# Prompt keys and values of a hybrid decoder layer: from TensorE transposes to VectorE squares and reordering stores

## The chip, the cores and the metric

The kernel runs on one core of one Trainium2 chip. A core has five engines that each work through their own list of instructions in order: TensorE (PE, with its weight loads as PEld), VectorE (DVE), ScalarE (ACT), GpSimd (POOL) and SyncE (SP). SP computes nothing here; it issues nearly all transfers, which then run on the core's 16 DMA engines. The metric is the device time of one execution in microseconds. Three timed runs of the kernel before took 1741.89 to 1742.96 us, with a median of 1742.4 us.

## The reference, cut to what matters

One decoder layer runs over a prompt of 1024 tokens and a sample of 8 sequences with 4 new tokens each, in one program (1056 tokens). From the normalised input a projection makes, among others, the stick-breaking q, k and v (8 heads of 64), the DeltaNet inputs and two gates. The prompt's keys and values are used by attention and are also outputs.

```python
def decoder_layer(x, ...):                          # once for the prompt, once for the sample
    p = rmsnorm(x, norm_mix_w) @ w_in
    q_a, k_a, v_a, u, z, a, b, g_a, g_b = jnp.split(p, ...)
    o_a = sb_prompt(q_a, k_a, v_a, sb_bias)         # w[q,k] = beta * product of (1-beta) after k; o = w @ v
    o_b, ssm_new = gdn_branch(short_conv(u_ext, conv_w), z, a, b, ...)   # gated delta rule, 4 heads
    m = sigmoid(g_a) * (o_a @ w_pa) + sigmoid(g_b) * (o_b @ w_pb)
    x = x + m @ w_o
    x = x + square(relu(rmsnorm(x, norm_mlp_w) @ w_up)) @ w_down
    return x, k_a, v_a, conv_new, ssm_new
# outputs, among others: k_a and v_a of the prompt as (page of 128 tokens, token, head, 64)
```

## The kernel before

Activations lie transposed in SBUF: features on the 128 partitions, tokens along the free dimension. Float32 products are made from a rounded part and a remainder of each factor, so that `dense` (L134) issues three matmuls (L137, L138, L139) for each 128 rows of the sum. `load_w` (L118) fetches 128 columns of weights through a staging tile that exists once (`wst`), and ACT and DVE split it into two tiles of which two pairs exist.

The front half of the program, up to some 890 us, has these parts in the text: four DeltaNet heads (`gdn_head`, L379), each with its projections, a chain through small transfers to DRAM and back (`ms_d` at L454, L456; 31 steps on DVE at L464; `tv_d` at L467, L471) and eight dependent chunks (L538, matmuls y, s, o); the sample's DeltaNet step; the projections of stick-breaking q, k and v (loop at L783, pair of heads p by pair, evacuated by `ev`, L793); the sample's attention (L854: scores dsc, transposed weights dwt, values dav, and dos, whose result `osT` is stored at L906); and the prompt's attention (`pipeline`, L1028), whose first stage `stage_a` loads a head's q and k (`attn_load`, L914) and, for every second head, v (`load_v`, L964), and makes scores (sc). Gate projections (pd_g, `gate_steps`, L1037; 16 jobs of 4 chunks with 24 matmuls each) and the transposed residual input (xrp, `residual_step`, L1046) are work that depends on none of these. Eleven gate jobs are written ahead of attention, the other five as fill between its blocks. After that come the merge, the output projection and the channel mixer, from some 890 us to the end.

The order on each engine is not the order of the text. A scheduler builds the program with a time model of its own and takes, engine by engine, what is ready first, within the limits of the pools: a tile's next user waits for the last reader of the buffer it takes over. The list of each engine is then fixed. Two such limits matter here. The projections of q, k, v, the gates and xrp share two PSUM tiles (`psf`, through `dtile(..., True)`) that are handed on in the order of the text, so gate chunk 1 of the job g1_5 can't be placed before the residual xrp0, which stands ahead of it. And attention's tiles (pool `ak`, L911) take the place of the sample's (pool `bk`, closed at L907), so they can't be filled before the sample's attention is over. SP's list is in order too: a transfer that waits for something holds up every transfer behind it.

For k and v of each pair p, the projection leaves a tile f of 128 features x 1024 tokens. Eight TensorE transposes (`tr8`, L367) turn it into two PSUM tiles t_nk or t_nv, ACT copies these into `nt` (L809), and SP stores `nt` to the output (L811) and, for v, once more to the scratch tensor `v_d` (L813), from which `load_v` reads later.

Of the kernel before, what the change touches and what calls it, by code (L numbers as in the profile page):

```python
# [8 lines left out]
F32 = mybir.dt.float32  # L9
# [9 lines left out]
P = 128  # L19
D = 1024  # L20
NP = 1024
# [17 lines left out]
def hybrid_step(ctx, tc, x_prompt, x_sample, cache_k, cache_v, page_table, state_conv, state_ssm,  # L39
# [24 lines left out]
    def dtile(name, f=False):  # L64
        if f:
            return psf.tile([P, 512], F32, tag="f", name=name)
        return psd.tile([P, 512], F32, tag="d", name=name)
# [80 lines left out]
    z_d = dr.tile([GH, P, NP], F32, name="z_d")  # L148
    q_d = [dr.tile([4, P, NP], F32, name=f"q{x}_d") for x in "hl"]
    k_d = [dr.tile([4, P, NP], F32, name=f"k{x}_d") for x in "hl"]  # L150
    v_d = dr.tile([4, P, NC, P], F32, name="v_d")
    cg_d = dr.tile([GH, NC, P], F32, name="cg_d")
    ms_d = dr.tile([GH, 4, NC, 32, 32], F32, name="ms_d")
    tv_d = dr.tile([GH, 4, NC, 32, 32], F32, name="tv_d")
# [221 lines left out]
    def c8(ap):  # L376
        return ap.rearrange("p (c f) -> p c f", f=P)
# [405 lines left out]
    for p in range(4):  # L783
        for nm, col, keep_s in (("q", 0, qsT), ("k", 512, ksT), ("v", 1024, vsT)):
            hi = lo = f = None
            if nm != "q":
                f = fk.tile([P, T], F32, tag="ft", name=f"{nm}f{p}", bufs=NFT)
            if nm != "v":
                hi = fk.tile([P, NP], F32R, tag="ft", name=f"{nm}h{p}", bufs=NFT)
            if nm == "q":  # L790
                lo = fk.tile([P, NP], F32, tag="ft", name=f"{nm}l{p}", bufs=NFT)

            def ev(c, o, n, pt, f=f, hi=hi, lo=lo, keep_s=keep_s[:, p, :]):  # L793
                m = min(n, NP - o)
                with tc.high_priority():
                    if hi is not None:
                        S_.activation(hi[:, o:o + m], pt[:, :m], AF.Copy)
                    if lo is not None:
                        V.tensor_tensor(lo[:, o:o + m], pt[:, :m], hi[:, o:o + m].bitcast(F32), op=ALU.subtract)
                    if f is not None:  # L800
                        S_.activation(f[:, o:o + m], pt[:, :m], AF.Copy)
                    if m < n:
                        V.tensor_copy(keep_s, pt[:, m:n])

            proj([(col + p * P, f"a{nm}{p}", ev)], f=True)
            if nm != "q":
                nt = fk.tile([P, NP], F32, tag="ft", name=f"nt{nm}{p}", bufs=NFT)
                for hf, pt in enumerate(tr8(f, f"n{nm}{p}", lambda n_: dtile(n_, True))):
                    S_.activation(nt[:, hf * 512:(hf + 1) * 512], pt, AF.Copy)  # L809
                dst = nk_prompt if nm == "k" else nv_prompt  # L810
                SY.dma_start(dst[0, 0, :, :, 2 * p:2 * p + 2, :].rearrange("c t h d -> t c (h d)"), c8(nt))  # L811
                if nm == "v":
                    SY.dma_start(v_d[p], c8(nt))  # L813
            if nm == "k":
                lo = f[:, 0:NP]
                V.tensor_tensor(lo, lo, hi.bitcast(F32), op=ALU.subtract)
            if nm != "v":
                for dst, src in zip(q_d if nm == "q" else k_d, (hi.bitcast(F32), lo)):
                    SY.dma_start(dst[p], src)
# [143 lines left out]

    def load_v(p):  # L964
        vn = ak.tile([P, NC, P], F32, tag="vn", name=f"vn{p}", bufs=2)
        SY.dma_start(vn, v_d[p])
        return vn

    def values_of(blk):
# [39 lines left out]
    def stage_a(x):  # L1009
        if x >= NB:  # L1010
            return
        hh, _ = blks[x]
        if hh not in heads:
            if hh // 2 not in vns:
                vns[hh // 2] = load_v(hh // 2)
            heads[hh] = attn_load(hh)
        state[x] = scores(blks[x])

    def stage_b(x, fill):
# [648 lines left out]
```

## Time and profile before

| | us |
|---|---|
| timed runs, median of three (lowest to highest) | 1742.4 (1741.89 to 1742.96) |
| the profiled execution | 1736.88 |
| its span, from the first to the last instruction | 1735.2 |
| mean granted TensorE clock | 0.993 of full speed |
| PE busy | 1689.5 (97% of the span) |
| DVE busy | 1143.6 (66%) |
| ACT busy | 781.7 (45%) |
| POOL busy | 198.2 (11%) |

Rows of the profile name an instruction by its line, its engine, its operation and `out<-in` with the program's tile names. "Idle before, releaser" is the time in which an engine stood still ahead of an instruction and what ended it. A matmul's own duration (some 280 ns) is longer than the distance to the next one, since they overlap; the distance is what the work costs.

### The profile page before, as it was taken

To read this page: it belongs to the slowest core of one execution; us is meant where nothing else is said; L and a number is where in the kernel's file an instruction comes from. 1 tells how busy PE (TensorE), PEld (TensorE's weight loads), DVE (VectorE), ACT (ScalarE), POOL (GpSimd) and SP (SyncE) were. 2 spreads that over 40 slices of the span, in tenths; PEclk is the share of its full clock that TensorE was granted. 3 is DMA by queue.
4 is the path that set the end of the run, shared out by engine and by line. 5 is a ranking of instruction groups with operands and counts; after the bars stand their busy time and mean duration, and the time that the engine had idled before them with its cause. 6 is when DMAs were issued, how large, how long until landed. Compare 5 with 4: busy or idle time off the path is not lost.

```text
span 1735.2 us, 34777 instructions
## 1 busy us (share of the span) xinstructions
PE 1689.5 (97%) x14030; PEld 1631.0 (94%) x14030; DVE 1143.6 (66%) x2300; ACT 781.7 (45%) x1560; POOL 198.2 (11%) x243
## 2 busy tenths in 40 slices
PE   7999999999999989999999999999999999999998
PEld 6999999999998778887989999999999999999998
DVE  6665677867243317558757487887776778788843
ACT  5453434343324225545433356554445564344353
POOL 2110111110005214335200000000000000000000
PEclk9999999999999999999999999999999999999999
DMA  5132233234446576748134644545443666442321
GB/s 179 37 120 76 68 106 92 85 119 135 123 132 216 149 194 172 194 124 241 57 113 126 184 139 144 158 133 160 151 155 113 235 220 214 155 132 94 122 81 66
DMA packets 234220, 239.24 MB, mean 138 GB/s; under 512 B 22882, under 2 KB 192195, under 8 KB 234060
## 3 DMA queue, kind: packets, MB, share of 16 engines
q1 hardware_dynamic: 229110, 226.27, 43.0%
q0 software_dynamic: 3200, 10.52, 1.9%
q8 instruction: 110, 1.80, 0.4%
q10 hardware_dynamic: 1750, 0.23, 0.1%
q14 instruction: 50, 0.41, 0.1%
HBM read 163.21 MB, written 73.77 MB: 137 GB/s over the span
## 4 chain that ended last, share of the span: by engine, by line
PE 77%; DVE 6%; issue 6%; DMA 6%; POOL 3%; ACT 2%; SPq 0%; POOLq 0%; DVEq 0%; ACTq 0%
PE pu L139 6%; PE pu L137 6%; PE pu L138 6%; PE pw L139 4%; PE pw L138 4%; PE pw L137 4%; PE pd_g L137 2%; PE pd_g L139 2%; PE pd_g L138 2%; POOL am L943 2%; PE px L138 1%; PE px L137 1%; PE px L139 1%; PE pv L139 1%; PE pv L137 1%
## 5 line engine op out<-in xcount | busy, mean ns | idle before, releaser
L139 PE MATMUL pu<-Xh,ul 128*128 128x264 f32 x812 | 230.1, 284 | 0.0
L137 PE MATMUL pu<-Xh,uh 128*128 128x264 f32 x812 | 229.8, 283 | 0.3 <-ACT uh L1231 0.3
L138 PE MATMUL pu<-Xl,uh 128*128 128x264 f32 x812 | 229.7, 283 | 0.0
L137 PE MATMUL pw<-hc,w 128*128 128x264 f32 x728 | 205.9, 285 | 2.4 <-ACT w L1480 2.4
L138 PE MATMUL pw<-hc,w 128*128 128x264 f32 x728 | 206.1, 286 | 0.0
L139 PE MATMUL pw<-hc,w 128*128 128x264 f32 x728 | 201.3, 285 | 0.2 <-DVE w L1481 0.2
L137 PEld LDWEIGHTS pu<-Xh,uh 128*128 128x128 f32 x812 | 153.1, 189 | 0.5 <-ACT uh L1231 0.5
L138 PEld LDWEIGHTS pu<-Xl,uh 128*128 128x128 f32 x812 | 152.7, 188 | 0.0
L139 PEld LDWEIGHTS pu<-Xh,ul 128*128 128x128 f32 x812 | 152.0, 188 | 0.0
L137 PE MATMUL pd_g<-xh,wh_g 128*128 128x256 f32 (+1 forms) x512 | 150.4, 294 | 0.0
L139 PE MATMUL pd_g<-xh,wl_g 128*128 128x256 f32 (+1 forms) x512 | 149.1, 291 | 0.0
L138 PE MATMUL pd_g<-xl,wh_g 128*128 128x256 f32 (+1 forms) x512 | 148.7, 290 | 0.0
L137 PEld LDWEIGHTS pw<-hc,w 128*128 128x128 f32 x728 | 138.0, 190 | 2.7 <-ACT w L1480 2.6
L138 PEld LDWEIGHTS pw<-hc,w 128*128 128x128 f32 x728 | 137.3, 189 | 0.0
L139 PEld LDWEIGHTS pw<-hc,w 128*128 128x128 f32 x728 | 134.6, 188 | 0.4 <-DVE w L1481 0.4
L947 DVE TENSOR_TENSOR_SCAN pr<-am 128x127 f32<-128x127 f32 (+7 forms) x64 | 88.0, 1376 | 62.5 <-POOL am L943 62.4
L139 PEld LDWEIGHTS pd_g<-xh,wl_g 128*128 128x128 f32 x512 | 97.5, 190 | 3.1 <-issue 2.9
L137 PEld LDWEIGHTS pd_g<-xh,wh_g 128*128 128x128 f32 x512 | 97.6, 191 | 2.9 <-issue 2.1
L138 PEld LDWEIGHTS pd_g<-xl,wh_g 128*128 128x128 f32 x512 | 97.4, 190 | 1.0 <-issue 0.8
L1480 ACT ACTIVATE w<-a 128x512 fp32r<-128x512 f32 x78 | 43.4, 620 | 85.9 <-PE pw L139 77.6
L139 PE MATMUL px<-mh,wl_wo 128*128 128x264 f32 x256 | 72.3, 285 | 1.2 <-DVE wl_wo L1232 1.1
L138 PE MATMUL px<-ml,wh_wo 128*128 128x264 f32 x256 | 72.6, 285 | 0.0
(579 smaller groups left out, 5083.4 us busy)
## 6 DMA issues: line engine op xcount, KB each, us to landing
hc_d<-t SPq DMA_DIRECT2D x26, 924.0 KB, 4.2
hc<-hc_d SPq DMA_DIRECT2D x87, 264.0 KB, 3.7
a<-in_w_down_dram SPq DMA_DIRECT2D x48, 256.0 KB, 5.8
ws_g<-in_w_in_dram SPq DMA_DIRECT2D x16, 512.0 KB, 6.6
ws_wo<-in_w_o_dram SPq DMA_DIRECT2D x32, 256.0 KB, 4.4
ua<-in_w_up_dram SPq DMA_DIRECT2D x16, 512.0 KB, 4.3
ub<-in_w_up_dram SPq DMA_DIRECT2D x16, 512.0 KB, 5.9
gA_d<-gt SPq DMA_DIRECT2D x8, 528.0 KB, 6.5
```

The source lines that it names most:

```text
L137: PE.matmul(pt[:, :n], lhsT=wh[k], rhs=xh[k], start=(k == 0), stop=False)
L138: PE.matmul(pt[:, :n], lhsT=wh[k], rhs=xl[k], start=False, stop=False)
L139: PE.matmul(pt[:, :n], lhsT=wl[k], rhs=xh[k], start=False, stop=(k == nk - 1))
L943: G.tensor_scalar(am[:, :n], s[:, :n], -1.0, 1.0, op0=ALU.mult, op1=ALU.add)
L947: V.tensor_tensor_scan(pr[:, n - 1:0:-1], am_r, am_r, 1.0, op0=ALU.mult, op1=ALU.bypass)
L1480: S_.activation(tl[:, 0], src, AF.Copy)
```

## The change

For each of the eight k and v tiles the TensorE transposes and the ACT copies go. One DVE instruction transposes every 32 x 32 square of f in its place, into `nt`. Four stores, one for each group of 32 features, then carry the squares' rows of 32 numbers (128 bytes) into a scratch tensor `n_d`, 1024 tokens x 128 features. The output is filled by a copy from `n_d` in DRAM, and `load_v` reads from `n_d` as well; the store to `v_d` is gone. In `stage_a` the loads of q and k now stand ahead of the load of v.

```diff
-    v_d = dr.tile([4, P, NC, P], F32, name="v_d")
+    n_d = {x: dr.tile([4, NP, P], F32, name=f"n{x}_d") for x in "kv"}
...
                 nt = fk.tile([P, NP], F32, tag="ft", name=f"nt{nm}{p}", bufs=NFT)
-                for hf, pt in enumerate(tr8(f, f"n{nm}{p}", lambda n_: dtile(n_, True))):
-                    S_.activation(nt[:, hf * 512:(hf + 1) * 512], pt, AF.Copy)
+
+                V.transpose(nt, f[:, 0:NP])
+                for a in range(4):
+                    SY.dma_start(n_d[nm][p].rearrange("(b i) f -> i b f", i=32)[:, :, 32 * a:32 * a + 32],
+                                 nt[32 * a:32 * a + 32].rearrange("i (b j) -> i b j", j=32))
                 dst = nk_prompt if nm == "k" else nv_prompt
-                SY.dma_start(dst[0, 0, :, :, 2 * p:2 * p + 2, :].rearrange("c t h d -> t c (h d)"), c8(nt))
-                if nm == "v":
-                    SY.dma_start(v_d[p], c8(nt))
+                SY.dma_start(dst[0, 0, :, :, 2 * p:2 * p + 2, :].rearrange("c t h d -> (c t) (h d)"), n_d[nm][p])
...
         vn = ak.tile([P, NC, P], F32, tag="vn", name=f"vn{p}", bufs=2)
-        SY.dma_start(vn, v_d[p])
+        SY.dma_start(vn, n_d["v"][p].rearrange("(c t) f -> t c f", t=P))
...
         if hh not in heads:
+            heads[hh] = attn_load(hh)
             if hh // 2 not in vns:
                 vns[hh // 2] = load_v(hh // 2)
-            heads[hh] = attn_load(hh)
```

The scheduler makes new lists from this text. Three places show what becomes of them (line numbers of the changed program are one higher from L815 on).

SP's list around the k tile of pair 2 (ntk2). kh_d and kl_d take q/k parts for attention, ms_d and ms3 belong to the chain of DeltaNet head 3, ws_ are weights for projections. Before:

```order
L454 DMA ms_d_141<-E13_3897 32x8x32 x4
L456 DMA ms3_3955<-ms_d_141 32x1024
L819 DMA kh_d_137<-kh2_5579 128x1024
L123 DMA ws_ak3_5960<-in_w_in_dram 128x8x128
L811 DMA out_2_dram<-ntk2_5695 128x8x128
L819 DMA kl_d_138<-kf2_5578 128x1024
L123 DMA ws_av3_6093<-in_w_in_dram 128x8x128
```

and with the change:

```order
L820 DMA kh_d_137<-kh2_5550 128x1024
L123 DMA ws_ak3_5916<-in_w_in_dram 128x8x128
L811 DMA nk_d_139<-ntk2_5666 32x32x32 x4
L820 DMA kl_d_138<-kf2_5549 128x1024
L814 DMA out_2_dram<-nk_d_139 1024x128
L454 DMA ms_d_142<-E13_3898 32x8x32 x4
L456 DMA ms3_3956<-ms_d_142 32x1024
L123 DMA ws_av3_6042<-in_w_in_dram 128x8x128
```

The copy to the output waits for the four stores to land, and head 3's chain, which stood ahead of this tile, now stands behind that wait.

PE's list from the second group of the sample's attention (dsc1) to the start of the prompt's attention (sc0). Lines of "..." leave out matmuls of gate chunks and repeats. Before:

```order
L867 MATMUL dsc1_6324<-kts4_6328,qbd_6251 32x260
...
L111 MATMUL dwt1_6433<-ident_119,ds1_6421 128x128 x2
...
L896 MATMUL dav1_6441<-vg4_6390,dw1_6437 32x512
...
L903 MATMUL dos1_6456<-sel_6233,om1_6454 128x16 x4
...
L137 MATMUL pd_g0_5_3_7672<-xh3_167,wh_g0_5_7590 128x288
...
L937 MATMUL sc0_0_0_7711<-kh0_7702,qs0_7701 128x128
...
L111 MATMUL xrp0_0_7855<-ident_119,xr0_7853 128x128 x4
...
L137 MATMUL pd_g1_5_1_7893<-xh1_171,wh_g1_5_7796 128x256
```

and with the change:

```order
L137 MATMUL pd_g0_5_3_7613<-xh3_168,wh_g0_5_7531 128x288
...
L868 MATMUL dsc1_6265<-kts4_6269,qbd_6192 32x260
...
L111 MATMUL dwt1_6374<-ident_119,ds1_6362 128x128 x2
L897 MATMUL dav1_6382<-vg4_6331,dw1_6378 32x512
...
L904 MATMUL dos1_6397<-sel_6174,om1_6395 128x16 x4
L938 MATMUL sc0_0_0_7652<-kh0_7641,qs0_7640 128x128
...
L111 MATMUL xrp0_0_7796<-ident_119,xr0_7794 128x128 x4
...
L137 MATMUL pd_g1_5_1_7834<-xh1_172,wh_g1_5_7737 128x256
```

Gate chunks that stood behind dsc1 (from the last chunk of g0_4 to the end of g0_5, nine chunks, and 14 matmuls of g1_5_0) now stand ahead of it; behind dsc1 nine gate matmuls are left until the first scores. From the matmul pd_g1_5_1 on, both lists are the same but for a few neighbours.

SP's list at the same place, where the prompt's attention begins (o_d<-osT is the store at L906, qs, kh, kl and vn are the loads of head 0, xr0 the residual input). Before:

```order
L906 DMA o_d_130<-osT_6261 128x4x32
L966 DMA vn0_7699<-v_d_139 128x1024
L923 DMA qs0_7701<-qh_d_135 64x1024
...
L925 DMA kl0_7703<-kl_d_138 64x1024
L1049 DMA xr0_7853<-in_x_prompt_dram 128x1024
L923 DMA qs1_7928<-qh_d_135 64x1024
...
L123 DMA ws_g0_6_8150<-in_w_in_dram 128x8x128
```

and with the change:

```order
L123 DMA ws_g0_6_8091<-in_w_in_dram 128x8x128
...
L123 DMA ws_g1_6_8431<-in_w_in_dram 128x8x128
L907 DMA o_d_130<-osT_6202 128x4x32
L924 DMA qs0_7640<-qh_d_135 64x1024
...
L926 DMA kl0_7642<-kl_d_138 64x1024
L967 DMA vn0_7649<-nv_d_140 128x8x128
L1050 DMA xr0_7794<-in_x_prompt_dram 128x1024
```

The load of v went behind head 0's q and k, and the weights of the next two gate jobs went from behind the attention loads to ahead of them.

## The prediction

> **What bounds the kernel now.** I read the page first, then the busy time by stage, then what TensorE (PE) waits for.
>
> ```profile
> PE 1689.5 (97%) x14030; PEld 1631.0 (94%) x14030; DVE 1143.6 (66%) x2300; ACT 781.7 (45%) x1560; POOL 198.2 (11%) x243
> ```
>
> PE is busy 97% of the span, so work taken from PE is worth its time wherever PE has no hole, and nothing where the hole only gets longer. The stages tell which is which (columns: length, then busy time of PE, PEld, DVE, ACT, POOL; granted clock, DMA share, GB/s):
>
> ```profile
> 100.00:460.00 360.00, 355.85 (x3195) 349.59 (x3196) 249.97 (x629) 143.04 (x332) 36.57 (x35) 1.00 0.34 101
> 460.00:513.00 53.00, 53.00 (x441) 53.00 (x441) 13.56 (x34) 15.42 (x48) 1.97 (x3) 1.00 0.28 84
> 513.00:620.00 107.00, 103.63 (x906) 87.67 (x904) 40.80 (x113) 33.49 (x67) 35.54 (x35) 0.97 0.62 186
> 620.00:648.00 28.00, 21.19 (x166) 20.72 (x166) 4.38 (x7) 6.19 (x13) 1.83 (x5) 0.95 0.92 229
> 648.00:890.00 242.00, 238.81 (x1945) 210.28 (x1945) 162.23 (x176) 124.75 (x270) 92.48 (x124) 0.99 0.54 147
> ```
>
> The changed tiles are made at 160 to 454 us, where PE stands still for 4 of 360 us. The next hole is at 620 to 648 us, where the prompt's attention begins: PE idle for 7 us, DMA share 0.92. PE's waits from 100 us on name both:
>
> ```profile
> PE t_nk L111 <- ACT ntk L809: 1.7, 2, 1.0
> PE t_nv L111 <- ACT ntv L809: 0.7, 1, 0.7
> ...
> PE dkt L111 <- DMA kg<-in_cache_k_dram,idx: 3.4, 1, 3.4
> ...
> PE sc L937 <- ACT s L939: 6.8, 1, 6.8
> ```
>
> The first two belong to the removed transposes, the third to the sample's attention, the last is the hole at 640 us.
>
> **Part one: what goes, and what takes its place.**
>
> ```profile
> 245.06 0.87 PE t_v L111 x8
> ...
> L809 ACT ACTIVATE ntk<-t_nk x8: 594/598/600, 162.8 to 434.9; 128x512 f32<-128x512 f32 x8
> ...
> L484 DVE STREAM_TRANSPOSE U<-t x4: 1239/1246/1246, 161.2 to 426.3; 128x1024 f32<-128x1024 f32 x4
> ...
> L811 SPq DMA_DIRECT2D out_dram<-ntk x4: 388/389/443, 178.4 to 435.6; - x4
> ...
> L813 SPq DMA_DIRECT2D v_d<-ntv x4: 484/1454/1814, 246.1 to 453.8; - x4
> ...
> L454 SPq DMA_DIRECT2D ms_d<-E x16: 303/442/1570, 104.2 to 383.7; - x16
> ...
> DMA to landing us min/median/max: 1.6/1.7/3.2
> ```
>
> Eight transposes of the same shape cost the chain 0.87 us, so the 64 that go are worth 8 x 0.87 = 7.0 us of PE, and the two waits for ACT's copies go with them: 1.7 + 0.7 = 2.4 us. Sum: -9.4 us. ACT loses 16 copies of 0.6 us; it was busy 143 of 360 us, so that is worth nothing. DVE gains eight square transposes; the one of this shape that the trace shows (U) takes 1.25 us, together 10 us more on the 250 of 360. They are covered by DVE's idle 110 us; with that cover gone each would delay a weight split behind it by 1.25 us.
>
> SP issues per tile four stores of 1024 rows of 128 bytes and one copy, in place of one or two stores. The trace has no such store. Nearest are ms_d (256 rows of 128 bytes: issue 0.44 us, landing after 1.7 us) and the stores of 1024 rows of 512 bytes (0.39 us for the first, up to 1.81 us for the one right behind it). So the copy can be issued after 4 x 0.44 + 1.7 = 3.5 us at least and 4 x 1.81 + 3.2 = 10.4 us at most; I take 6.5 us, between the two, since the row length is that of ms_d and the row count that of v_d. Behind it on SP wait weights and the transfers of the DeltaNet heads, first of all head 3's (ms_d, then tv_d). The tightest place is the k tile of pair 3: counted in PE's list, 175 matmuls at 0.12 us, 21 us, lie between the end of its projection and the first matmul (l1) that needs head 3's inverse. In that time must pass the square transpose (1.25), a store of tv (0.4 + 1.7), four loads of the ms_d kind (3.5) and the transpose U (1.25), some 8.5 us with the evacuation. That leaves 12 us for the stores, more than the upper bound, so I take their price on the path as zero.
>
> The Trainium skill, "DMA: Bandwidth & Descriptors", section Specifications, speaks against this part: below 512 bytes a transfer misses line rate because of read-modify-write. If that doubled the landing, the upper bound would be 13.6 us, 1.6 us more than the room. In this trace ms_d, which writes rows of 128 bytes, lands in 1.7 us and shows no such price.
>
> **Part two: what the new order does.** The 9.4 us arrive only if PE finds work up to the next fixed point. The lists show that it doesn't. Attention's tiles can't be filled before the sample's attention is over, so between dsc1 and the first scores there is a chain: scores, weights, values, osT, then loads. Before, 250 matmuls fill that time, nearly all of them gates; now 44, of which 9 are gates. The missing ones stand ahead of dsc1, where they were not needed as cover. Both lists meet again at the matmul pd_g1_5_1, and behind it they are practically the same; so the time of that matmul decides. Rows of before, timeline and chain:
>
> ```profile
> 603.10 1.96 PE L867 MATMUL dsc<-kts,qbd 128*32 128x260 f32 x32
> ...
> 607.36 0.17 DVE L881 TENSOR_TENSOR wx<-sgrp,ds 128x16 f32<-128x16 f32 x1
> ...
> 609.82 0.38 PE L111 MATMUL dwt<-ident,ds 128*128 128x128 f32 x2
> ...
> 616.06 0.69 DVE L900 TENSOR_TENSOR om<-dav,m 128x512 f32<-128x512 f32 x1 [5.48 <-PE dav L898]
> ...
> 619.11 0.96 PE L903 MATMUL dos<-sel,om 128*128 128x16 f32 x8
> ...
> 620.36 0.36 SPq L906 DMA_DIRECT2D o_d<-osT  x1
> ...
> 620.89 0.38 SPq L966 DMA_DIRECT2D vn<-v_d  x1
> ...
> 625.97 0.44 SPq L925 DMA_DIRECT2D kl<-kl_d  x1
> 626.51 0.70 SPq L1049 DMA_DIRECT2D xr<-in_x_prompt_dram  x1
> ...
> 633.47 0.39 SPq L123 DMA_DIRECT2D ws_g<-in_w_in_dram  x1
> ...
> 645.83 1.06 ACT L127 ACTIVATE wh_g<-ws_g 128x1024 fp32r<-128x1024 f32 x1 [8.62 <-DMA ws_g<-in_w_in_dram]
> ...
> 649.69 0.56 PE L137 MATMUL pd_g<-xh,wh_g 128*128 128x256 f32 x1
> ```
>
> Before, dsc1 starts at 603.1, osT is stored at 620.4, and pd_g1_5_1 runs at 649.7 us, held back by gate weights (ws_g) that were issued behind 13 loads and that ACT needed first. The change issues them earlier, so that hole closes; but a new one opens ahead of it.
>
> Step 1, start of dsc1. Nine more gate chunks and 14 matmuls come ahead. A chunk costs what lies between two evacuations:
>
> ```profile
> 630.04 0.38 ACT L1042 ACTIVATE gt<-pd_g 128x256 f32<-128x256 f32 x1 [2.46 <-PE pd_g L139]
> 632.89 0.38 ACT L1042 ACTIVATE gt<-pd_g 128x256 f32<-128x256 f32 x1 [2.46 <-PE pd_g L139]
> 636.08 0.41 ACT L1042 ACTIVATE gt<-pd_g 128x288 f32<-128x288 f32 x1 [2.81 <-PE pd_g L139]
> ```
>
> 2.85 us (of 256 columns, 0.119 a matmul) and 3.19 us (of 288): 6 x 2.85 + 3 x 3.19 + 14 x 0.119 = 28.4 us. The wait for kg shrinks: 18 more matmuls, 2.1 us, stand between the last DeltaNet chunk and that place. I take -2; at best all 3.4 us go, and the half clock after them (below), some 2 us: -5.5. So dsc1 starts at 603.1 + 28.4 - 9.4 - 2 = 620.1 us.
>
> Step 2, dsc1 to the store of osT: 17.2 us before. In it PE was late twice: dwt 2.3 us behind wx, dos 2.4 us behind om's end, both in line behind gates. Bounds 12.5 and 17.2; I take 14.5, near the low end since the gates are gone: 634.6 us.
>
> Step 3, the loads. PE's list has xrp0 ahead of pd_g1_5_1, so q, k of head 0 (6 x 256 KB), vn0 and xr0 (512 KB each) must be there: 2.6 MB at the 229 GB/s of this stage, 11.4 us, plus 0.5 us to the first issue and 1.7 us to land: 648.2 us. At the 290 GB/s shown below 8.8 us, with a landing of 3.2 us 13 us later.
>
> Step 4, from there to pd_g1_5_1: eight transposes and three short pieces, at half clock. After a hole PE runs at half speed:
>
> ```profile
> 544.00:548.00 4.00, 0.63 (x8) 0.34 (x3) 0.00 (x0) 0.00 (x0) 1.51 (x2) 0.80 0.99 290
> 548.00:552.00 4.00, 4.00 (x34) 2.49 (x34) 0.61 (x1) 1.19 (x2) 1.09 (x2) 0.50 0.20 70
> ...
> 640.00:644.00 4.00, 0.59 (x5) 0.35 (x3) 0.00 (x0) 0.00 (x0) 0.00 (x0) 1.00 1.11 238
> 644.00:648.00 4.00, 0.59 (x1) 0.50 (x2) 1.08 (x1) 2.17 (x4) 0.57 (x1) 0.67 0.56 222
> 648.00:652.00 4.00, 4.00 (x20) 3.79 (x19) 3.10 (x4) 1.89 (x5) 3.74 (x6) 0.50 0.75 165
> ```
>
> So 2 x 0.87 + 1.1 = 2.8 us: 651.0 us, 1.3 us later than before. The half clock lasts on a little: before, to 652 us; now the hole is longer (some 20 us with little in it), I add 1.2 us, bounds 0 and 3.4. **Sum: +2.5 us.** The profiled execution took 1736.88 us (span 1735.2 us) and would take 1739.4; the median of the three runs lies 5.5 us above it at 1742.4, so the forecast for a median is **1744.9 us**. The gain is real on PE and is spent in a longer wait where attention begins. All low ends together give dsc1 at 616.6, +12.5, +0.5 + 8.8 + 1.7, +2 = 642.1 us, -7.6 us; all high ends 622.1 + 17.2 + 0.5 + 11.4 + 3.2 + 3 + 3.4 = 660.8, +11 us.
>
> **The rivals.** A: the gain stays. The chain and the loads take their low ends and the wait for kg goes: -7.6 us, 1734.8 us. For it speak the 97% of PE and a DMA system that has shown 290 GB/s; against it that several low ends must meet. B, on the other side: SP's list blocks. If the four stores and their landing take more than the 12 us of room, because each issue waits for the rows of the one ahead, the DeltaNet chain of head 3 comes late at the k tiles of pairs 2 and 3 and PE, in order, stands. At twice the issue price, 4 x 3.6 + 3.2 = 17.6 us, that is 5.6 us at two places: 1744.9 + 11 = 1756 us. For it speaks v_d's 1.81 us behind a store of as many rows; against it that those rows were four times as long. C: DVE becomes the bound, each square transpose in front of a weight split that PE needs: at most 8 x 1.25 = 10 us, 1755 us; against it DVE's 110 idle us and weights that are split a projection ahead.
>
> **How the numbers follow.** What can be told from no change here is about 0.2%, 3.5 us. The forecast's case has 0.56: its own range of -4 to +8 us gives 0.10 faster, 0.28 the same, 0.18 slower. A has 0.17 (0.16 faster, 0.01 the same), B 0.22 (0.21 slower, 0.01 the same), C 0.05 (0.04 slower, 0.01 the same). Together faster 0.26, same 0.31, slower 0.43. The range goes from A's 1735 to B's 1756 us.
>
> **What would show it.** Right: no t_nk or t_nv on PE and no waits for them; the stage up to dsc1 fully busy, dsc1 at about 620 us; then a PE hole of 15 to 20 us between dsc1 and xrp0, ended by transfers, and no ACT wait for ws_g behind it; SP free again 4 to 10 us after a tile. Wrong: dsc1 well after 625 us with PE waiting for l1 or y of head 3 (B) or for weight splits by DVE (C), or pd_g1_5_1 before 646 us (A). A second change of place, outside attention's start, would break the argument that the lists meet there.

## The result, and the profile of the changed kernel

The change makes the kernel slower. It took 1757.5 us (median of four runs, 1755.3 to 1759.8) beside 1742.1 us for the kernel before: ratio 1.0086, 95% interval 1.0071 to 1.0102, some 15 us. Measured once more it stood at 1.0077 (1.0052 to 1.0101). Forecast were 1744.9 us and a range up to 1756.

The profiled execution has a span of 1753.6 us, 18.4 us more than before, at a mean clock of 0.987 (before 0.993). That is 3 us more than the timed runs differ by: the execution profiled for the kernel before, 1736.88 us, lies some 5 us below its timed runs (the section on the experiments says how chips differ). First line of its page, then the stages (columns as in the prediction):

```profile
PE 1692.8 (97%) x13966; PEld 1630.4 (93%) x13966; DVE 1154.7 (66%) x2308; ACT 779.6 (44%) x1547; POOL 198.5 (11%) x243
```

```profile
100.00:460.00 360.00, 353.09 (x3152) 348.08 (x3151) 257.10 (x626) 137.12 (x315) 37.49 (x35) 1.00 0.41 107
460.00:513.00 53.00, 52.32 (x439) 51.72 (x440) 11.55 (x24) 16.98 (x46) 0.00 (x0) 1.00 0.28 81
513.00:620.00 107.00, 101.54 (x849) 91.08 (x848) 43.27 (x120) 32.70 (x69) 27.65 (x27) 0.95 0.57 169
620.00:648.00 28.00, 22.66 (x184) 14.47 (x182) 5.59 (x16) 6.85 (x15) 10.41 (x10) 0.88 0.48 145
648.00:680.00 32.00, 21.24 (x128) 17.63 (x128) 14.13 (x16) 11.22 (x24) 12.46 (x16) 0.73 0.86 199
```

PE issues 64 matmuls fewer, 7 us, and is nevertheless busy 3.3 us longer: more of its work ran at half clock (0.993 - 0.987 of some 1750 us is 10.5 us). And it is idle for 1753.6 - 1692.8 = 60.8 us instead of 45.7. The idle time grew where the tiles are made (6.9 of 360 us, before 4.1) and most of all from 620 us on, where attention begins. PE's waits from 100 to 700 us:

```profile
PE sc L938 <- DMA kh<-kh_d: 9.7, 1, 9.7
PE dwt L111 <- DVE ds L879: 4.4, 1, 4.4
PE dkt L111 <- issue: 3.0, 1, 3.0
PE pd_aq L137 <- DVE vsT L803: 1.8, 1, 1.8
PE pd_g L137 <- DVE vsT L803: 1.5, 1, 1.5
PE pd_g L139 <- issue: 1.5, 2, 1.1
PE l L522 <- ACT x L520: 0.8, 1, 0.8
```

The waits for t_nk and t_nv are gone with the transposes; in their place stand waits for VectorE (vsT, the last piece of a v projection's evacuation, now queued behind other work of that engine) and, at attention's start, for the chain of the sample's attention (dwt) and its successor, the loads of q and k (sc). The timeline there:

```profile
633.68 1.52 PE L868 MATMUL dsc<-kts,qbd 128*32 128x260 f32 x24
...
641.30 0.66 PE L111 MATMUL dwt<-ident,ds 128*128 128x128 f32 x2 [4.41 <-DVE ds L879]
...
649.78 0.36 SPq L907 DMA_DIRECT2D o_d<-osT  x1
...
659.22 0.77 PE L938 MATMUL sc<-kh,qs 128*128 128x128 f32 x2 [9.73 <-DMA kh<-kh_d]
...
664.34 1.97 PE L111 MATMUL xrp<-ident,xr 128*128 128x128 f32 x8
...
667.44 0.28 PE L137 MATMUL pd_g<-xh,wh_g 128*128 128x256 f32 x1
```

The last row is pd_g1_5_1, where both lists meet: 667.4 us, 17.75 us after its place in the kernel before (649.69). Of the 18.4 us of span all but 0.6 have arisen by then.

What came late earlier on is head 3 of the DeltaNet: its inverse goes out to DRAM (tv_d), comes back and is transposed (U), and eight dependent chunks follow (o). Before, then after:

```profile
L467 SPq DMA_DIRECT2D tv_d<-tv x1: 334/334/334, 417.8 to 417.8; - x1
L484 DVE STREAM_TRANSPOSE U<-t x1: 1246/1246/1246, 426.3 to 426.3; 128x1024 f32<-128x1024 f32 x1
L558 PE MATMUL o<-st,cgb x56: 275/275/275, 199.6 to 502.9; 128*128 128x128 f32 x56
```

```profile
L467 SPq DMA_DIRECT2D tv_d<-tv x1: 375/375/375, 435.3 to 435.3; - x1
L484 DVE STREAM_TRANSPOSE U<-t x1: 1246/1246/1246, 445.4 to 445.4; 128x1024 f32<-128x1024 f32 x1
L558 PE MATMUL o<-st,cgb x56: 275/275/275, 201.7 to 528.0; 128*128 128x128 f32 x56
```

U starts 19 us later and the last chunk 25 us later. Half of the 19 us is there when the chain begins, with the store of E (ms_d). Before, then after:

```profile
L454 SPq DMA_DIRECT2D ms_d<-E x4: 319/442/449, 382.3 to 383.7; - x4
L454 SPq EVENT_SEMAPHORE  x1: 17/17/17, 382.3 to 382.3; - x1
```

```profile
L454 SPq DMA_DIRECT2D ms_d<-E x4: 303/443/452, 392.2 to 393.5; - x4
L454 SPq EVENT_SEMAPHORE  x1: 3371/3371/3371, 388.8 to 388.8; - x1
```

The store is 9.9 us later, and SP stood 3.4 us waiting for E, which VectorE makes: SP's list, with its copy ahead of the chain, did not hold it up here. Another 5 us are added in the 31 steps on VectorE (L464), between which two of the square transposes now run: from the first to the last 34.6 us instead of 29.7. The remaining 4 us lie in the issue and landing of the chain's transfers. PE hardly waits for U or the chunks, since the new list puts gate chunks ahead: 564 gate matmuls between the end of the projections of q, k and v and the last chunk, 339 before. These are the chunks that are missing behind dsc1.

### The profile page after: what moved, and what is told of

Read it like the earlier page. It is cut to its first block, busy times and chain, and to the rows that moved or that the text cites. A ratio compares the mean times of both kernels' runs of the same rounds, so it can differ in the third digit from the quotient of the medians.

```text
span 1753.6 us, 34685 instructions
## 1 busy us (share of the span) xinstructions
PE 1692.8 (97%) x13966; PEld 1630.4 (93%) x13966; DVE 1154.7 (66%) x2308; ACT 779.6 (44%) x1547; POOL 198.5 (11%) x243
## 3 DMA queue, kind: packets, MB, share of 16 engines
q10 hardware_dynamic: 1750, 0.23, 0.1%
## 4 chain that ended last, share of the span: by engine, by line
PE 84%; DMA 7%; DVE 4%; issue 2%; SPq 2%; ACT 2%; DVEq 0%; POOLq 0%; ACTq 0%
PE pu L139 6%; PE pu L137 6%; PE pu L138 6%; PE pw L139 4%; PE pw L138 4%; PE pw L137 4%; PE pd_g L137 4%; PE pd_g L139 4%; PE pd_g L138 3%; PE po L986 2%; PE wt L111 2%; PE px L138 1%; PE pv L137 1%; PE pv L139 1%; PE px L137 1%
## 5 line engine op out<-in xcount | busy, mean ns | idle before, releaser
L940 ACT ACTIVATE s<-sc,sbb 128x512 f32<-128x512 f32 (+3 forms) x96 | 53.2, 581 | 44.5 <-PE sc L939 33.1
```

The source lines that it names most:

```text
L940: S_.activation(s[:, k0:k0 + kn_], pt[:, :kn_], AF.Sigmoid, bias=sbb[:, hh:hh + 1], scale=HD ** -0.5)
```

## The experiments

The two theories at the start: **order**, by which the time goes where the new list spends its gate chunks before they are needed as cover; and **stores**, by which the four short-row stores and the copy hold up SP or the transfers behind them. Kernels of a batch shared a chip, and the kernel before took about 1735.6 us on some chips and 1742 on others, so ratios are compared, each against the kernel before on its own chip. 0.001 is 1.7 us. e1 to e4 and e13 to e16 ran on chips of the first kind, the change and e5 to e12 on chips of the second. Only the kernel before ran on both, so that the chip's share is the same for all kernels is assumed, not shown; a difference across the kinds (e1 and e9, e11 and e13, e3 and the change) is weaker than one within them.

The trace of the kernel before fits the first kind by its time (1736.9 us, where the first kind's runs took 1732 to 1740 us and the second's 1740 to 1750), and the trace of the change is of the second. How much that is can be read from e9, which has the old PE list place by place and ran on the second kind: its dsc1 starts at 605.1 us (before 603.1) and its xrp0 at 644.9 us (640.0). So up to 5 of the 18.4 us may be the chip's. The late dsc1 is the chip's in part at most: e3 and e4, with the change's list up to that place and on the first kind, have it at 633.5 and 627.6 us, the change at 633.7; e11 and e14, alike on PE beyond that place, have it at 630.6 on the second kind and 627.8 on the first.

| run | edit | ratio to before | 95% interval |
|---|---|---|---|
| the change | | 1.0086 | 1.0071 to 1.0102 |
| e5 | the change again | 1.0077 | 1.0052 to 1.0101 |
| e1 | TensorE transposes kept, new stores | 1.0036 | 1.0024 to 1.0049 |
| e6 | e1, copies deferred | 1.0047 | 1.0029 to 1.0064 |
| e9 | e1, one store of 512-byte rows | 0.9994 | 0.9982 to 1.0007 |
| e10 | e1, transfers on POOL's queue | 1.0064 | 1.0041 to 1.0088 |
| e2 | change, nine gate chunks held | 1.0085 | 1.0068 to 1.0102 |
| e3 | change, residual later | 1.0037 | 1.0023 to 1.0051 |
| e4 | change, swap of the loads undone | 1.0133 | 1.0114 to 1.0151 |
| e7 | change, copies deferred | 1.0089 | 1.0062 to 1.0116 |
| e8 | e7, residual later, four chunks held | 1.0066 | 1.0043 to 1.0089 |
| e12 | change, POOL's queue, residual later | 1.0026 | 1.0007 to 1.0044 |
| e11 | change, one store of 512-byte rows | 1.0051 | 1.0030 to 1.0073 |
| e13 | no transposes at all, one store | 1.0034 | 1.0021 to 1.0046 |
| e14 | e11, residual later | 1.0007 | 0.9995 to 1.0019 |
| e15 | before, residual later | 1.0001 | 0.9987 to 1.0015 |
| e16 | e15 and the swap | 1.0005 | 0.9994 to 1.0016 |

**The stores alone.** e1 keeps the TensorE transposes and with them PE's list, but for the places between 357 and 430 us where matmuls of the projections and of DeltaNet alternate:

```diff
-                V.transpose(nt, f[:, 0:NP])
+                for hf, pt in enumerate(tr8(f, f"n{nm}{p}", lambda n_: dtile(n_, True))):
+                    S_.activation(nt[:, hf * 512:(hf + 1) * 512], pt, AF.Copy)
                 for a in range(4):
-                    SY.dma_start(n_d[nm][p].rearrange("(b i) f -> i b f", i=32)[:, :, 32 * a:32 * a + 32],
-                                 nt[32 * a:32 * a + 32].rearrange("i (b j) -> i b j", j=32))
+                    SY.dma_start(n_d[nm][p].rearrange("(c t) f -> t c f", t=P)[:, :, 32 * a:32 * a + 32],
+                                 c8(nt)[:, :, 32 * a:32 * a + 32])
```

> The change with its transposes undone: TensorE transposes and ScalarE copies as before, but the four stores of 128-byte rows into n_d, the copy from DRAM to the output and load_v from n_d as in the change. PE's list is then that of the kernel before, place by place (564 - 339 gate matmuls are not moved ahead of DeltaNet's end). Theory (order: the time is lost where gate work is spent before the sample's attention, not in the stores): same as before, 1742 us, -2 to +4, dsc1 at 603 to 606 us. Rival (SP: four stores and the copy hold up what stands behind them): 4.7 to 9.4 us from the first store to the copy at eight tiles, dsc1 5 to 13 us later, 1747 to 1757 us.

Measured 1.0036, 6.3 us: the rival's figure, not the theory's, though dsc1 started at 605.3 us, where the theory had it and not the rival. The new stores cost time without the change's new order. Its trace, head 3's chain, PE's wait for it, and the landing of the stores (KB each, median us):

```profile
L467 SPq DMA_DIRECT2D tv_d<-tv x1: 328/328/328, 426.0 to 426.0; - x1
L484 DVE STREAM_TRANSPOSE U<-t x1: 1247/1247/1247, 434.4 to 434.4; 128x1024 f32<-128x1024 f32 x1
```

```profile
PE l L493 <- DVE U L484: 2.3, 1, 2.3
```

```profile
nk_d<-ntk SPq DMA_DIRECT2D x16, 128.0 KB, 4.9
nv_d<-ntv SPq DMA_DIRECT2D x16, 128.0 KB, 3.1
```

U is 8.1 us late and PE, in the old order, stands 2.3 us for it; the rest of the 6.3 us stands in no row of PE's waits. Three edits of e1 ask what of the stores it is. e6 takes the copies out of the way, by holding them on SP behind attention's second load of v:

```diff
-                SY.dma_start(dst[0, 0, :, :, 2 * p:2 * p + 2, :].rearrange("c t h d -> (c t) (h d)"), n_d[nm][p])
+                outs.append((dst[0, 0, :, :, 2 * p:2 * p + 2, :].rearrange("c t h d -> (c t) (h d)"), n_d[nm][p]))
...
     pipeline(0, SPLIT, fills)
+    with tc.issue_after(vq[1].ins):
+        for dst, src in outs:
+            SY.dma_start(dst, src)
```

e10 issues the four stores and the copy of each tile from POOL (`G.dma_start` for `SY.dma_start`). e9 makes one store of the four:

```diff
-                for a in range(4):
-                    SY.dma_start(n_d[nm][p].rearrange("(c t) f -> t c f", t=P)[:, :, 32 * a:32 * a + 32],
-                                 c8(nt)[:, :, 32 * a:32 * a + 32])
+                SY.dma_start(n_d[nm][p].rearrange("(c t) f -> t c f", t=P), c8(nt))
```

> As e1_pe_transposes_new_stores (TensorE transposes, four stores of 128-byte rows, PE's list as before), but the eight copies from DRAM to the output wait on SP until attention's second load of v is issued, some 80 us behind the place where the sample's attention ends, so that nothing on SP waits for the stores to land. e1 stood 6.3 us above before (ratio 1.0036), with head 3's DeltaNet inverse U 8 us late. If the copy's wait on SP is the price: U at 426 to 429 us, ratio 0.999 to 1.0015. If the price is the four stores themselves (2.2 to 5.4 us of issue a tile) : U stays at 431 us or later, ratio 1.003 to 1.005.

> As e1 (TensorE transposes, four stores of 128-byte rows, the copy from DRAM, PE's list as before), but all 40 transfers are issued from POOL's queue instead of SP's. If what the stores cost is that SP's list is held up (2.2 to 6.8 us of issue a tile): U at 426 to 429 us, ratio 0.999 to 1.0015. If the cost lies in the DMA engines, which the 128-byte rows keep from the small transfers of head 3's chain (tv_d to t took 4.0 us in e1 instead of 2.0): U stays at 432 us or later, ratio 1.003 to 1.005.

> TensorE transposes and ScalarE copies as before, PE's list as before; per tile one store of 512-byte rows into n_d instead of four of 128-byte rows, then the copy from DRAM to the output, load_v from n_d. Against e1 and e6 (ratios 1.0036 and 1.0047) only the form of the store differs. If the four stores of short rows are the price: head 3's U at 426 to 430 us, ratio 0.999 to 1.0015. If the price is the second pass through DRAM (the copy, 4 MB more of traffic): ratio 1.003 to 1.005.

e6 stays at 1.0047 with U at 434.7 us (e1: 434.4): U isn't late for the copy's wait. e10 is no better (1.0064, U at 438.8 us), but it doesn't price SP's list: POOL has work of the chain itself, and the chain's first store comes 8 us later than in e1 (393.1 us instead of 385.0). e9 is at 0.9994, and its chain is that of the kernel before:

```profile
L467 SPq DMA_DIRECT2D tv_d<-tv x1: 335/335/335, 418.0 to 418.0; - x1
L484 DVE STREAM_TRANSPOSE U<-t x1: 1246/1246/1246, 426.6 to 426.6; 128x1024 f32<-128x1024 f32 x1
```

So the detour through DRAM costs nothing, and by the ratios the four stores of 128-byte rows cost 1.0036 - 0.9994 = 0.0042, 7 us. e1 and e9 are of different kinds of chip, and their two traces don't show these 7 us (spans of 1739.0 and 1739.3 us); on the second kind e6 and e10, both with short rows, stand 0.0053 and 0.0070 above e9, with other differences besides. By which way they delay the chain stays open: in e1 the load of ms was issued at 388.30 us, behind half a megabyte of weights, and its first reader started 4.9 us later; in e9 it was issued at 385.57 us, ahead of them, since the scheduler changed SP's list too, and the reader started 2.1 us later. The steps on VectorE then took longer as well (32.4 us from the first to the last instead of 29.8). A run with short rows and SP's old list wasn't made.

**The list.** e2 holds the missing chunks back, on PE alone:

```diff
-    for j, b in gjobs[:11]:
-        for f in gate_steps(j, b):
-            f()
+    for x, (j, b) in enumerate(gjobs[:11]):
+        for c, f in enumerate(gate_steps(j, b)):
+            with tc.issue_after(dsc_last.ins) if 4 * x + c >= 35 else ExitStack():
+                f()
```

> The change, with the last nine gate chunks (the last of g0_4, all of g1_4 and g0_5) held behind the last matmul of dsc1 on PE; all else as in the change. Behind dsc1 stand then 216 gate matmuls before the first scores instead of 9 (before: 215). Theory (order): 207 matmuls of 0.119 us, 24.6 us, move into a stage that had 16 us of PE idle and some 24 us at half clock between 634 and 668 us; 10 to 20 us come back: 1738 to 1748 us. Rival (the late gather: what binds is the sample's keys, kg, which start 28 us later than before): between the first transposed key and dsc0 then stand 72 gate matmuls instead of 230, PE waits there for the gathers instead, and the time stays at 1752 to 1760 us with the idle time ahead of dsc1.

1.0085, no gain by the ratios, as the rival said: the hole goes to where the sample's keys are transposed. Its stage there, idle for 4.4 of 24 us and at half clock:

```profile
580.00:604.00 24.00, 19.57 (x75) 8.88 (x75) 12.11 (x28) 3.77 (x9) 2.12 (x3) 0.54 0.45 128
```

Moving chunks back only moves the hole, for those ahead of dsc1 were covering something as well. e3 takes new fill instead, gate chunks that stood behind the residual:

```diff
-            if t % 2 == 0 and t // 2 < 9:
-                fills.append(lambda t=t // 2: residual_step(t))
+            if t >= 4 and t % 2 == 0 or t == 19:
+                fills.append(lambda t=min(t - 3, 16) // 2: residual_step(t))
```

> The change, with the residual steps among the fill starting four gate chunks later, so that the chunks of g1_5 no longer wait for xrp0 in the two shared PSUM tiles. PE's list up to dsc1 is that of the change; behind it 105 gate matmuls stand before the first scores instead of 9. Theory (order): 72 to 96 matmuls of 0.119 us fill idle time between dsc1 and the first scores: -8.6 to -11.4 us, and half clock is shorter: 1743 to 1749 us, with dsc1 at 633 us as in the change. Rival (the loads set the end of the hole and something later takes the gain, as DVE's scans or the gates' weights): 1754 to 1760 us.

1.0037 against 1.0077 and 1.0086 for the change; the intervals do not meet. About 7 us come back. The stretch from dsc1 on, of the change (e5) and of e3:

```profile
634.00:690.00 56.00, 39.31 (x268) 29.13 (x268) 24.29 (x31) 16.75 (x37) 24.02 (x29) 0.79 0.81 201
```

```profile
634.00:690.00 56.00, 45.58 (x324) 36.20 (x317) 26.24 (x30) 18.07 (x40) 25.54 (x29) 0.85 0.78 197
```

PE gets 6.3 us more done in the same 56 us, at a better clock. The missing fill is a real part of the loss. The change itself ran on the other kind of chip than e2, e3 and e4, so the size rests on the ratios; on e3's own chip e2 and e4 are slower, and e13 and e14 below show the effect of the same edit on one chip.

e4 undoes the last part of the diff:

```diff
-            heads[hh] = attn_load(hh)
             if hh // 2 not in vns:
                 vns[hh // 2] = load_v(hh // 2)
+            heads[hh] = attn_load(hh)
```

> The change, with load_v ahead of the loads of q and k again, as before. Theory (order): vn0 is 512 KB of 2.6 MB that must land before xrp0 in either order; the first scores come 2 us later, the end does not move: 1756 to 1760 us. Rival (the new order of the loads is what costs): 1745 to 1752 us.

e4 is at 1.0133, slower than either theory expected: the first scores waited 12.0 us for kh instead of 9.7. So there is no sign that the swap is part of the loss. Whether it saves anything isn't settled: the change beside it is of the other kind of chip, the 8 us of the ratios aren't explained by these 2.3 us, and in the old order (e16 less e15, one chip) the swap does nothing.

> The change as it is, beside the kernel before on the same chip as the three runs that follow, so that they can be compared with it. Both theories: the ratio to before is 1.007 to 1.010 as in its first measurement (1.0086); with that, e4_swap_undone (1.0133) would stand as slower than the change, and a ratio of 1.011 or more here would say that the swap alone does nothing.

1.0077, as expected. e7 is the change with e6's edit, e8 is e7 with e3's edit and with e2's for the chunks of g0_5 alone (`>= 40`), e12 the change with e10's and e3's.

> The change with the same deferral of the eight copies, transposes on VectorE as in the change. PE's list then has 33 gate matmuls fewer ahead of DeltaNet's end and 38 more between dsc1 and the first scores (47 instead of 9). Order and head 3's chain as the cause: 38 x 0.119 = 4.5 us of fill come back and the chain is 2 to 4 us earlier, dsc1 at 626 to 630 us, 4 to 9 us less than the change: ratio 1.0035 to 1.0065. If only what stands at attention's start counts and the copies cost nothing: 1.007 to 1.010.

1.0089, a miss for the first theory and in the second one's range: U starts only 1.2 us earlier than in the change (444.2 us), and the 38 matmuls of fill bring nothing that stays, while xrp, with the copies now among attention's loads, waits 3.7 us for xr.

> The change with three repairs: copies deferred (as e7), the residual steps four chunks later (as e3), and the last four gate chunks (g0_5) held behind dsc1. Behind dsc1 stand then 183 gate matmuls before the first scores, the 231 between the first transposed key and dsc0 stay. If the two causes add up (fill at attention's start -8 to -12 us as in e3, copies -4 to -6): ratio 0.997 to 1.002, the hole between dsc1 and the first scores under 6 us. If the sample's keys or the loads bind instead: 1.003 to 1.006.

1.0066, a miss, probably for the same reason: its longest wait is for the same load, and the DMA share there is 1.07.

```profile
PE xrp L111 <- DMA xr<-in_x_prompt_dram: 5.0, 1, 5.0
```

```profile
660.00:700.00 40.00, 34.99 (x268) 30.16 (x267) 25.66 (x26) 19.98 (x44) 22.05 (x28) 0.96 1.07 279
```

> The change with its stores and copies issued from POOL's queue and with the residual steps four gate chunks later (as e3), as a version that might beat the kernel before. PE's list: 44 gate matmuls fewer ahead of DeltaNet's end than in the change, 143 instead of 9 gate matmuls between dsc1 and the first scores. If SP's list is the price of the stores, both repairs add up: 0.996 to 1.001. If the stores cost on any queue: 1.002 to 1.005, like e3.

1.0026, as expected if the stores cost on any queue: the lowest of the variants that do all that the change does, and still slower than the kernel before.

**VectorE or the order.** e11 has the change's VectorE transposes with one store:

```diff
-                for a in range(4):
-                    SY.dma_start(n_d[nm][p].rearrange("(b i) f -> i b f", i=32)[:, :, 32 * a:32 * a + 32],
-                                 nt[32 * a:32 * a + 32].rearrange("i (b j) -> i b j", j=32))
+                SY.dma_start(n_d[nm][p].rearrange("(c t) f -> t c f", t=P), c8(nt))
```

The squares are then not put into place. e13 drops `V.transpose` as well and stores `f` itself, so that nothing is transposed; on PE the gate chunks stand as in e11, while the matmuls of the projections and of DeltaNet alternate otherwise up to 460 us:

```diff
-                V.transpose(nt, f[:, 0:NP])
-                SY.dma_start(n_d[nm][p].rearrange("(c t) f -> t c f", t=P), c8(nt))
+                SY.dma_start(n_d[nm][p].rearrange("(c t) f -> t c f", t=P), c8(f[:, 0:NP]))
```

> The change, but each tile is stored with one transfer of 512-byte rows, which leaves out the putting into place of the squares: the keys and values read from n_d stand in wrong places, the work is otherwise the same. PE's list stands between: 44 gate matmuls fewer ahead of DeltaNet's end than the change, 47 instead of 9 gate matmuls between dsc1 and the first scores. If order and stores each have their share: 1.002 to 1.005. If the stores are the whole loss, PE's 7 us are gained: 0.995 to 1.000. If the order is the whole loss: 1.006 to 1.009.

> As e11, and VectorE's transposes are left out too: the tile f is stored as it is, with one transfer of 512-byte rows, so that keys and values are not transposed at all. PE's list is the one of e11, place by place. If the new order is what costs (DeltaNet's end 117 matmuls later in the list than before, 47 gate matmuls of fill at attention's start instead of 215): the same as e11 (1.0051), 1.003 to 1.0065, although 64 transposes on PE and 8 on DVE are gone and nothing stands for them. If VectorE's transposes are what costs (PE waited 2.8 us for vsT behind them in e11): 0.995 to 1.001.

e11 is at 1.0051, e13 at 1.0034. This is the clearest run: with 64 matmuls taken from PE and nothing put in their place on any engine, the program is 6 us slower than the kernel before on the same chip. The 7 us that PE no longer works don't show at the end, and the list that the scheduler makes of the lighter program costs more than they are worth. VectorE's transposes are by the ratios 0.0017 or 3 us, across the kinds of chip and with intervals that overlap, so nothing and 7 us are both possible. In the traces U starts at 444.2 us with them and at 430.1 without, and DeltaNet ends at 526 and 519 us; the 31 steps of head 3 take 34.0 us with them and 29.9 without.

```profile
L484 DVE STREAM_TRANSPOSE U<-t x1: 1245/1245/1245, 430.1 to 430.1; 128x1024 f32<-128x1024 f32 x1
L558 PE MATMUL o<-st,cgb x56: 275/275/275, 197.0 to 518.6; 128*128 128x128 f32 x56
```

```profile
PE sc L934 <- DMA kh<-kh_d: 9.6, 1, 9.6
```

The last row is e13's longest wait: the same hole in front of the first scores as in the change, without transposes and short stores.

> As e11 (VectorE transposes, one store of 512-byte rows, squares not put into place), with the residual steps four gate chunks later as in e3: 143 gate matmuls stand between dsc1 and the first scores instead of 47. If the missing fill is the loss: 96 x 0.119 = 11 us come back, ratio 0.998 to 1.001. If the loads or the sample's keys bind: 1.003 to 1.006.

e14 is e11 with e3's edit: 1.0007, in the range expected for the fill. Against e11, across the kinds of chip, 0.0044 or 8 us come back, of the 11 us reckoned. Against e13, on the same chip, e14 is 0.0027 faster and the intervals don't meet, although VectorE's transposes are back in it. So with the fill returned and one store, the program is level with the kernel before.

e14 also says more of VectorE's transposes, for its list up to dsc1 holds the same gate chunks as e13's, the rest alternating otherwise: dsc1 starts at 627.8 us, in e13 at 617.6. Of these 10.2 us 3.3 are there from the program's beginning (the first pd_z starts at 75.4 and 72.1 us). In this pair of executions the transposes thus delay dsc1 by some 7 us, more than the 3 us of the ratios.

**A version faster than both.** The fill repair might be a gain of its own: e15 is the kernel before with e3's edit, e16 that with the swap of the loads.

> The kernel before, with the residual steps four gate chunks later and nothing of the change. PE's list is that of before up to the first scores; SP issues the weights of the next gate job ahead of the residual's 512 KB, some 2 us earlier, and the hole at 640 us (6.8 us, ended by those weights) shrinks by as much. 0.9975 to 1.0000. If the hole only moves: 0.9995 to 1.002.

> As e15, and the loads of q and k stand ahead of the load of v, the one part of the change that is cheap. The first scores come 2 us earlier; PE's list is that of e15. If the hole at attention's start is set by the loads: 0.9965 to 0.9990, a version faster than both. If it is set by the gates' weights alone: as e15, 0.9975 to 1.0000.

1.0001 and 1.0005: no gain. Before has 250 matmuls at that place, and what is saved there (its wait for s fell from 6.8 to 4.8 us in all) is lost behind it. No run beat the kernel before.

## Why the prediction was wrong

The case that the forecast added up is e13: the new order, and neither VectorE's transposes nor short stores, which part one put at nothing. It cost 1.0034, 6 us, where 2.5 were forecast. Step 1's sum, with the 192 matmuls that e13's list moves ahead of dsc1, gives 603.1 + 192 x 0.119 - 9.4 - 2 = 614.5 us for dsc1, and the trace has 617.6. So the order was priced about rightly, and the change lost 7 to 9 us more (1.0077 and 1.0086 less 1.0034, across the kinds of chip) by what part one took as zero. On e13's own kind e2 and e4, with both terms in them, stand 0.0051 and 0.0099 above it. How the 7 to 9 us divide is open. By the ratios VectorE's transposes are 3 us (e11 less e13) and the stores 4.5 to 6 us (the change less e11; e1 less e9 gives 7), but the intervals overlap in both of the first pairs, and e11 and e13 are of different kinds of chip. By the traces, one execution each, VectorE's share is the larger one: e14 less e13 has 7 us of it at dsc1, while dsc1 in the change is 3.1 us later than in e11, on the same kind of chip, which the 38 more gate matmuls ahead of it (4.5 us) explain without the stores.

**Part one, VectorE's transposes and the stores taken as zero: this step failed.** The size of the stores was right: from the first store's issue to the copy's the trace shows 4.7 to 9.4 us, within the bounds of 3.5 and 10.4 and around the 6.5 that was taken. The room at the counted place held too: PE doesn't wait for l1 there. Wrong was to look at that place alone, with the chain's own pieces at their old prices, and to take VectorE's 110 idle us in 360 as cover for work that a chain has to pass. In the change the chain's steps on VectorE take 5 us longer and U is 19 us late, and up to the first transposed key PE has 4.6 us of waits ended by VectorE (vsT 3.3, st 0.8, qsT 0.5), where before it had 1.6. In e1 the stores alone, with no transposes on VectorE, make the chain 8.1 us later. The rule of the Trainium skill, "DMA: Bandwidth & Descriptors", section Specifications, was set aside because ms_d with rows of 128 bytes landed in 1.7 us. With 128 KB instead of 32 KB a store, e1 shows 4.9 and 3.1 us at the median. By the rule a loss was to be expected from rows below 512 bytes, and the ratios of e1 and e9 agree; that read-modify-write is the way, no run here shows.

**Step 1, dsc1 at 620.1 us: mis-sized by 13.6 us.** This is where part one's zeros show. dsc1 started at 633.7. The work ahead was counted rightly; what was wrong is what PE loses on the way. The stretch up to dsc1 before and after:

```profile
100.00:603.00 503.00, 495.47 (x4382) 476.67 (x4382) 300.43 (x766) 188.81 (x439) 70.08 (x68) 0.99 0.39 116
```

```profile
100.00:634.00 534.00, 520.95 (x4558) 502.31 (x4560) 315.20 (x777) 192.26 (x440) 71.31 (x68) 0.99 0.43 117
```

Idle before: 7.5 us. The step let 2.4 and 2 of them go, which leaves 3.1; measured are 13.0, so 10 us too few. Busy should have been 495.5 + 28.4 - 7.0 = 516.9 us and was 520.9: 4 us of half clock that wasn't reckoned with. Most of the idle time had arisen by the first transposed key (dkt): from 100 us on 8.3 us instead of the 4.2 - 2.4 = 1.8 that the step left there. The wait for kg, which was to shrink, grew as well: PE stood 3.0 us ahead of the ninth transposed key, at 566.7 us, and 2.4 us in shorter pieces just before (the trace names no releaser there, only "issue"), where before it stood 3.4 us ahead of the 26th. The gathers were issued 28 us later (548.6 instead of 520.8 us), like the first transposed key itself (557.1 instead of 528.7). The count of 18 matmuls more between DeltaNet and that key was about right (231 and 212 in the traces) and said nothing of the gathers' time.

**Steps 2 to 4 held.** dsc1 to osT took 16.1 us (taken 14.5, bounds 12.5 and 17.2). From there to xrp0 14.6 us (13.6), from xrp0 to pd_g1_5_1 3.1 us (2.8). The hole between dsc1 and xrp0 came, with 16 us of idle time from 634 to 668 us, of which transfers ended 10 and the chain of the sample's attention the rest, and ACT has no wait for ws_g behind it. That both lists meet at pd_g1_5_1 and nothing changes behind it held to 0.6 us.

**The rivals.** A (the gain stays) is out: e13 shows that it wouldn't stay even alone. B forecast 1756 us and came near the time, and its place, head 3's chain, is right; but that is luck, for its mechanism, SP's list blocked by landing waits, is not what the runs show: at the chain's start SP waited 3.4 us for VectorE and not the reverse, and without the copy's wait (e6) U is as late as with it. And in the change itself PE doesn't stand for l1 or y of head 3 (the two waits of 0.8 us above, for l and y, fall at 366.9 and 402.5 us, before head 3's U): the list has put gate chunks there, and the bill comes at attention's start. C, with its 10 us at most, was nearer than its chance of 0.05 says: the transposes cost 3 us by the ratios and 7 us at dsc1 by e13 and e14, though not in front of weight splits but in the steps of head 3's chain and in the evacuation of projections.

The deeper fault is that the forecast took the new list as the price of the change and then costed it row by row with the waits of the old one. DeltaNet's later end was in that list, to be read as nine chunks "ahead of dsc1"; that a chain which sets the start of the next stage, here the gathers, had itself become later was not asked.

## What to carry to other kernels

Work taken from a busy engine is worth its time only if the next fixed point isn't the end of a chain of latencies; ask of the new order not how many rows moved but which chain starts later, and what fill is left behind it. Idle time of an engine, taken over a long stretch, is no cover for work that lands in the middle of such a chain (the 31 steps took 34 us instead of 30). Where a scheduler makes the lists, test an edit with the lists kept (e9 keeps PE's place by place) and the lists with the edit taken out (e13): the shares come apart, if all of it runs on one kind of chip. In this program stores of short rows came with late small transfers of that chain, though their issue and landing seemed to fit.

## What the runs showed of the hardware

The clock fell in places without a hole. In the change PE was busy throughout from 600 to 612 us and was granted 0.74 and 0.84 in two of the three stretches:

```profile
600.00:604.00 4.00, 4.00 (x22) 2.62 (x20) 2.19 (x5) 1.35 (x2) 0.00 (x0) 1.00 0.04 16
604.00:608.00 4.00, 4.00 (x16) 2.71 (x15) 2.11 (x4) 0.00 (x0) 0.00 (x0) 0.74 1.00 267
608.00:612.00 4.00, 4.00 (x19) 2.62 (x18) 0.69 (x1) 0.57 (x2) 0.00 (x0) 0.84 0.01 4
```

What stands out there is the number of matmuls, 16 to 22 in 4 us, where a gate's stretch at full clock has some 33. Sparse use alone doesn't explain it, since the kernel before has as few at full clock:

```profile
572.00:576.00 4.00, 4.00 (x13) 1.49 (x12) 1.88 (x4) 0.00 (x0) 0.00 (x0) 1.00 0.10 16
576.00:580.00 4.00, 4.00 (x22) 2.14 (x20) 1.13 (x2) 0.00 (x0) 0.00 (x0) 1.00 0.00 0
```

The cause stays open. At attention's start the clock was 0.50 in all three 4-us stretches from 652 to 664 us, where the kernel before shows one such stretch, 648 to 652 us; so the hole also slowed the first work behind it.
